# Modulation of two transformer blocks: four of six weight thirds multiplied and added on VectorE, with one sum over the partitions on TensorE

## The chip, the cores and the metric

The kernel runs on one core of one Trainium2 chip. The metric is the device time of one execution in microseconds (us), from the launch of the program to its end. A span is the time from the first to the last instruction of a profiled execution, a little shorter than the execution's own time.

## What is computed

The program is two transformer blocks on 256 tokens of 1024 features, in float32. The first block is a gated feed-forward, an attention mixer and a second gated feed-forward. The second block is two layers over the token stream and a context stream of 256 tokens. Each of its layers has normalisations that are scaled and shifted by a modulation, three branches (Fourier, window attention and a gated recurrence), a gated merge of the branches, and a feed-forward with squared ReLU. The change touches the modulation:

```python
def modulation(cond, w, b):
    m = jax.nn.silu(cond) @ w + b
    return jnp.split(m, 6, axis=-1)

for l in range(DEPTH_2):
    mx = [m[:, None, :] for m in modulation(c, w_mod[l], b_mod[l])]
    mc = modulation(c_ctx, w_mod[l], b_mod[l])
    h = adaln_norm(x, norm1_g[l], mx[0], mx[1])
    ...
    x = x + mx[2] * y
    h2 = adaln_norm(x, norm2_g[l], mx[3], mx[4])
    x = x + mx[5] * sq_relu_mlp(h2, w_ff1[l], w_ff2[l])
```

For each of the two layers, two vectors of 1024 (one for the tokens, one for the context) are multiplied with a weight of 1024 x 6144. That is 25 MB of weights per layer that are read once, for two rows of output. The kernel splits the 6144 columns of a layer into three thirds of 2048 columns (r = 0, 1, 2), so there are six thirds (l, r).

## The kernel before

**The large products.** Every weight of the large matmuls comes in units of 128 partitions x 1024 elements. `wunit` (L230 to L237) loads a unit into `raw` on the queue of SyncE (SP), ScalarE (ACT) rounds it into `hi` (L235), and VectorE (DVE) subtracts to get the remainder `lo` (L236). Each of the three tiles has three buffers. `mm3` (L239 to L242) makes each product out of three matmuls on TensorE (PE): high times high, low of the weight and low of the activation in turn. A unit is 24 matmuls, of 512 columns where both streams are computed together and of 256 where only one is. A unit's `hi` buffer comes free when TensorE has finished the unit three places before it.

**The modulation.** `mods` (L670 to L701) is a generator that is given a list of thirds. A third is eight steps. A step loads 128 rows of the third, a tile `wm` of 128 x 2048 with two buffers (L679), and multiplies it by the 128 rows of silu(cond), padded from 2 to 32 columns in `csil32`. The 2048 columns are four quarters of 512, each a matmul of a 32-column block of the array (L681), and the eight steps add up in one PSUM bank. After the eighth step the bank is copied to SBUF (L686), transposed (L689), and added to the bias into `modt` (L691). Where it is needed, `derived` (L699) is made of it. `csil` holds the two vectors as 128 x 8 x 2.

**Where the steps stand.** The callers pull one step at a time between their own products, with `next(between, None)`. Third (0,0) runs in the first feed-forward, at about 60 us. Thirds (0,1) and (0,2) run in `merge` of layer 0 (L1303, L1318, L1332), which goes over n = 0, 1, 2 (the branches) and over jb = 0 to 3: for n = 0 and 1 a gate product of 2 units of 256 columns (the context's gate has been computed ahead), a branch product of 1 unit of 512 columns, and multiplications by the gate on VectorE (L888, L1337, L1339, L1340). The three thirds of layer 1 run in layer 0's feed-forward (L1395 to L1455), which is two halves hf, each a first product `w_ff1` (L1422, L1434) and a second, `w_ff2` (L1450). Two steps are pulled before the feed-forward and one or two at each unit pair of `w_ff1`.

**What lies between merge and feed-forward.** The product with `w_out` (L1385, L1390) is made for both streams for jb = 0, 1, and for the context (s = 1) and then the tokens (s = 0) for jb = 2, 3. As soon as a stream is done, its modulated normalisation `adaln` (L460 to L473) runs: the sum of squares on TensorE (L326, L357), VectorE and GpSimd for the reciprocal root (L365, L368), diagonals (L378, L380), a matmul that spreads them over the partitions (L381), and then for each of 8 feature blocks L469 and L472 on VectorE and L471 on ScalarE. The context's `adaln` runs while TensorE makes the `w_out` product of the tokens, and `w_ff1` begins with the context.

**The order.** The program is recorded in the order of the code, and a scheduler of the Tile framework then orders the instructions of each engine. Each engine works through its own queue in order. An instruction that waits holds up all that stands behind it on the same engine, and this holds for the DMA issues on SP's queue too.

## Time and profile before

| | |
|---|---|
| time, median of 3 runs | 2091.83 us (2088.09 to 2098.27) |
| the profiled execution's own time | 2091.31 us |
| its span | 2089.2 us |
| TensorE busy, matmuls | 2039.9 us |
| VectorE busy | 1292.0 us |
| ScalarE busy | 1060.4 us |
| moved by DMA | 328.04 MB, mean 157 GB/s |
| granted clock of TensorE | 0.991 |

The busy time of an engine is the time in which at least one of its instructions is at work. The granted clock is a share of full speed. A stretch is given below by its start and end in us from the span's start: the merge of layer 0 is 905 to about 1085, `w_out` and `adaln` 1085 to 1165, and its feed-forward 1129 to about 1500.

### The profile page before, as it was taken

Reading aid. Unit: us, or ns where it says so; the run is one execution under the profiler, and the core shown is the slowest. Engines: PE = TensorE matmul, PEld = TensorE weight load, DVE = VectorE, ACT = ScalarE, POOL = GpSimd, SP = SyncE. Lnnn points to the kernel's source line nnn. Section 1 sums busy time; section 2 is a strip of 40 time slices with the busy share of each in tenths; the row PEclk is TensorE's granted clock in tenths of the full one; section 3 lists DMA queues with packets and bytes.
Section 4 is the critical chain, followed back from the end, with each engine's and each line's share of the span. In section 5 each row is a group of like instructions: output and inputs, shape, how many; then the busy total and the mean of one; then the engine's idle time right before and its main releaser. Section 6 shows DMA issues by size and latency. Waiting matters only on the chain.

```text
span 2089.2 us, 34286 instructions
## 1 busy us (share of the span) xinstructions
PE 2039.9 (98%) x13959; PEld 1802.4 (86%) x13959; DVE 1292.0 (62%) x2011; ACT 1060.4 (51%) x1716; POOL 69.4 (3%) x63
## 2 busy tenths in 40 slices
PE   8999999999999999999999999999999999999999
PEld 8899988999999777888778778778898678999998
DVE  5575666865667699855456433343478897666654
ACT  5354455644446588664444331233266775555542
POOL 1111000111000000000000000000000000000000
PEclk9999999999999999999999999999999899999999
DMA  7886654566562211168535763342363123655564
GB/s 230 295 247 199 183 163 136 174 183 187 171 206 71 71 41 51 54 226 272 188 141 173 261 224 108 111 152 91 109 184 110 43 74 121 199 174 153 182 186 136
DMA packets 294687, 328.04 MB, mean 157 GB/s; under 512 B 18816, under 2 KB 282834, under 8 KB 287874
## 3 DMA queue, kind: packets, MB, share of 16 engines
q1 hardware_dynamic: 294530, 325.86, 49.7%
q8 instruction: 109, 1.79, 0.4%
q14 instruction: 48, 0.39, 0.1%
HBM read 318.40 MB, written 11.35 MB: 158 GB/s over the span
## 4 chain that ended last, share of the span: by engine, by line
PE 91%; DVE 3%; ACT 3%; DMA 1%; issue 1%; POOL 0%; SPq 0%; POOLq 0%; DVEq 0%; ACTq 0%
PE mx L240 14%; PE mx L242 14%; PE mx L241 14%; PE mm L240 12%; PE mm L242 12%; PE mm L241 12%; PE hg L1187 2%; PE ax L681 1%; PE at L1036 1%; PE ax L326 1%; PE mx L681 1%; PE at L1073 1%; PE at L1063 1%; PE at L240 1%; PE at L242 1%; PE at L241 1%
## 5 line engine op out<-in xcount | busy, mean ns | idle before, releaser
L236 DVE TENSOR_TENSOR lo<-raw,hi 128x1024 fp32r<-128x1024 f32 x478 | 584.8, 1225 | 511.0 <-ACT hi L235 507.0
L235 ACT CAST hi<-raw 128x1024 fp32r<-128x1024 f32 x478 | 497.3, 1041 | 716.1 <-PE mx L241 390.7
L240 PE MATMUL mx<-hh,hi 128*128 128x256 f32 (+1 forms) x1248 | 379.6, 304 | 1.2 <-ACT hh L400 1.2
L242 PE MATMUL mx<-hh,lo 128*128 128x256 f32 (+1 forms) x1248 | 376.9, 302 | 0.6 <-DVE lo L236 0.6
L241 PE MATMUL mx<-hl,hi 128*128 128x256 f32 (+1 forms) x1248 | 376.6, 302 | 0.5 <-DVE hl L401 0.5
L240 PE MATMUL mm<-hh,hi 128*128 128x256 f32 (+1 forms) x1136 | 371.7, 327 | 4.9 <-ACT z L1127 1.7
L242 PE MATMUL mm<-hh,lo 128*128 128x256 f32 (+1 forms) x1136 | 367.5, 324 | 1.5 <-DVE lo L236 1.5
L241 PE MATMUL mm<-hl,hi 128*128 128x256 f32 (+1 forms) x1136 | 365.9, 322 | 0.3 <-DVE hl L472 0.3
L240 PEld LDWEIGHTS mx<-hh,hi 128*128 128x128 f32 x1248 | 235.5, 189 | 25.4 <-ACT hi L235 6.7
L242 PEld LDWEIGHTS mx<-hh,lo 128*128 128x128 f32 x1248 | 236.4, 189 | 10.6 <-DVE lo L236 1.0
L241 PEld LDWEIGHTS mx<-hl,hi 128*128 128x128 f32 x1248 | 236.2, 189 | 10.4 <-DVE hl L401 0.8
L240 PEld LDWEIGHTS mm<-hh,hi 128*128 128x128 f32 x1136 | 215.3, 190 | 32.3 <-issue 7.4
L242 PEld LDWEIGHTS mm<-hh,lo 128*128 128x128 f32 x1136 | 215.2, 190 | 18.3 <-DVE lo L236 2.6
L241 PEld LDWEIGHTS mm<-hl,hi 128*128 128x128 f32 x1136 | 215.8, 190 | 16.4 <-issue 2.5
L240 PE MATMUL mx<-fh,hi 128*128 128x256 f32 (+1 forms) x368 | 120.3, 327 | 0.0
L241 PE MATMUL mx<-fl,hi 128*128 128x256 f32 (+1 forms) x368 | 120.3, 327 | 0.0
L242 PE MATMUL mx<-fh,lo 128*128 128x256 f32 (+1 forms) x368 | 120.2, 327 | 0.0
L240 PEld LDWEIGHTS mx<-fh,hi 128*128 128x128 f32 x368 | 69.2, 188 | 6.8
L241 PEld LDWEIGHTS mx<-fl,hi 128*128 128x128 f32 x368 | 69.2, 188 | 6.6
L242 PEld LDWEIGHTS mx<-fh,lo 128*128 128x128 f32 x368 | 69.4, 188 | 6.4
L1187 PE MATMUL hg<-qt,kt 128*128 128x128 f32 x384 | 62.0, 285 | 1.0 <-ACT dg L1194 0.5
L1187 PEld LDWEIGHTS hg<-qt,kt 128*128 128x128 f32 x384 | 55.2, 197 | 7.7 <-issue 2.1
(380 smaller groups left out, 3732.6 us busy)
## 6 DMA issues: line engine op xcount, KB each, us to landing
raw<-in_w_ff_dram SPq DMA_DIRECT2D x136, 512.0 KB
raw<-in_w_in_dram SPq DMA_DIRECT2D x130, 512.0 KB
wm<-in_w_mod_dram SPq DMA_DIRECT2D x48, 1024.0 KB
raw<-in_ffn_w_gate_dram SPq DMA_DIRECT2D x44, 512.0 KB
raw<-in_ffn_w_up_dram SPq DMA_DIRECT2D x44, 512.0 KB
raw<-in_ffn_w_down_dram SPq DMA_DIRECT2D x40, 512.0 KB
raw<-in_w_out_dram SPq DMA_DIRECT2D x28, 512.0 KB
raw<-in_w_qkv_dram SPq DMA_DIRECT2D x24, 512.0 KB
```

What stands on the lines that cost most here:

```text
L235: S.copy(hi, raw)
L236: V.tensor_tensor(out=lo, in0=raw, in1=hi.bitcast(F32), op=ALU.subtract)
L240: PE.matmul(ps, l[0], r[0], start=start, stop=False)
L241: PE.matmul(ps, l[0], r[1], start=False, stop=False)
L242: return PE.matmul(ps, l[1], r[0], start=False, stop=stop)
L326: PE.matmul(self.ss[:, t:t + 1], sq[:, i * T + t * P:i * T + (t + 1) * P], ones[:, :1], start=(first and i == 0 and t == 0), stop=(last an ...
L681: PE.matmul(ps[32 * c:32 * c + 32, :], cst_[:, k, :], wm[:, c * 512:(c + 1) * 512], start=(k == 0), stop=(k == KD - 1), tile_position=(0, ...
L1036: PE.matmul(scs[t], q[e][:, t * P:(t + 1) * P], kd[g][i][:, 512 - nk:], start=(i == 0), stop=(i == 1 and s == 1))
L1063: PE.transpose(pt[:, kt * T + t * P:kt * T + (t + 1) * P], sb[:, c0:c0 + P], ident)
L1073: mm = PE.matmul(op[e * 64:e * 64 + 64, :T], vt[:, vc:vc + 64], pts[e][:, kt * T:(kt + 1) * T], start=(ki == 0), stop=(ki == nk // P - 1))
L1187: PE.matmul(ps[:, (s * 2 + st) * P:(s * 2 + st + 1) * P], kt[:, s * T + st * P:s * T + (st + 1) * P], qt[:, s * T + tt * P:s * T + (tt + 1 ...
```

## The change

Each third in a list now has a flag. Without it the eight steps are matmuls as before. With it, a step is two VectorE instructions, one for each of the two vectors s: the first step multiplies `wm` by the vector's 128 values, one per partition, into an accumulator `macc` of 128 x 2048 (L700), and the seven others multiply and add to it in place (L702). After the eighth step two groups of four matmuls add the accumulators up over the 128 partitions, with a column of ones in `pick` that puts each vector's sum into its row (L686). Copy, transposes and bias are as before (now L710, L713, L715, L723). Thirds (0,2), (1,0), (1,1) and (1,2) have the flag; (0,0) and (0,1) have not.

The places at which steps are pulled change as well. In `merge` the second pull of a jb is at n = 0 alone, so that third (0,1) is done in n = 0, and third (0,2) has four steps in n = 1 and four in n = 2. In the feed-forward the two steps ahead of it and the four in the first `w_ff1` products are gone. One step is pulled at each of the six other unit pairs of the first half, three after each of the four jb of its `w_ff2`, and one at each of the first six pairs of the second half.

```diff
--- before.py
+++ after.py
@@ -667,21 +667,45 @@
     derived = [[[cp.tile([P, 8], F32, name=f"der{l}{s}{i}") for i in range(2)] for s in range(2)] for l in range(2)]
 
 
+
+    pick = cp.tile([P, 2, 32], F32, name="pick")
+    nc.gpsimd.memset(pick, 0.0)
+    for s in range(2):
+        nc.gpsimd.memset(pick[:, s, s:s + 1], 1.0)
+
     def mods(pool, parts, tag="ax"):
+
+
 
         cst_ = pool.tile([P, KD, 32], F32, tag="csil32", name="csil32")
         nc.gpsimd.memset(cst_, 0.0)
         nc.gpsimd.tensor_copy(cst_[:, :, 0:2], csil)
-        for l, r in parts:
-            ps = bank(tag)
+
+        def quarters(ps, stat, mov, first, final):
+            for c in range(4):
+                PE.matmul(ps[32 * c:32 * c + 32, :], stat, mov[:, c * 512:(c + 1) * 512], start=first, stop=final,
+                          tile_position=(0, 32 * c))
+
+        for l, r, dve in parts:
+            ps = None if dve else bank(tag)
+            acc = [pool.tile([P, 2048], F32, tag=f"macc{s}", name="macc") for s in range(2)] if dve else None
             for k in range(KD):
                 wm = pool.tile([P, 2048], F32, tag="wm", name="wm", bufs=2)
                 nc.sync.dma_start(out=wm, in_=a["w_mod_2"][l, k * P:(k + 1) * P, r * 2048:(r + 1) * 2048])
-                for c in range(4):
-                    PE.matmul(ps[32 * c:32 * c + 32, :], cst_[:, k, :], wm[:, c * 512:(c + 1) * 512],
-                              start=(k == 0), stop=(k == KD - 1), tile_position=(0, 32 * c))
+                if not dve:
+                    quarters(ps, cst_[:, k, :], wm, k == 0, k == KD - 1)
+                for s in range(2 if dve else 0):
+                    c = csil[:, k, s:s + 1]
+                    if k == 0:
+                        V.tensor_scalar(out=acc[s], in0=wm, scalar1=c, scalar2=None, op0=ALU.mult)
+                    else:
+                        V.scalar_tensor_tensor(out=acc[s], in0=wm, scalar=c, in1=acc[s], op0=ALU.mult, op1=ALU.add)
                 if k < KD - 1:
                     yield
+            if dve:
+                ps = bank(tag)
+                for s in range(2):
+                    quarters(ps, pick[:, s], acc[s], s == 0, s == 1)
             sb = tmp(512, "sq", 3)
             V.tensor_copy(sb, ps)
             pt = bank(tag)
@@ -768,7 +792,7 @@
         logc = btmp("sb")[:8, :]
         nc.sync.dma_start(out=logc, in_=a["c_logc"])
         nc.sync.dma_start(out=two(namask), in_=a["c_namask"])
-        steps = mods(bp, [(0, 0)])
+        steps = mods(bp, [(0, 0, False)])
         for _ in range(3):
             next(steps)
             yield
@@ -1300,7 +1324,7 @@
         mp = mg.enter_context(tc.tile_pool(name=f"mg{l}", bufs=1, reuse_waits="tile"))
         merged = mp.tile([P, 4 * ns, 512], F32, name="merged")
 
-        between = mods(mp, [(0, 1), (0, 2)]) if l == 0 else iter(())
+        between = mods(mp, [(0, 1, False), (0, 2, True)]) if l == 0 else iter(())
 
         def merge(n):
             parts = []
@@ -1329,7 +1353,7 @@
                         sigmoid_(e, g, -1.0)
                         sg.append(two(e))
                 pps = linear(a["w_branch_2"][l, n], 0, 4, jb * 256, bact, ntok)
-                if jb % 2:
+                if n == 0:
                     next(between, None)
                 for i, pr in enumerate(pps):
                     mu = two(merged[:, jb * len(pps) + i, :])
@@ -1392,10 +1416,7 @@
                 adaln(x, (s,), A2, B2, h, sums)
 
         fp = fs.enter_context(tc.tile_pool(name=f"ff{l}", bufs=1, reuse_waits="tile"))
-        between = mods(fp, [(1, 0), (1, 1), (1, 2)], "mx") if l == 0 else iter(())
-
-        for _ in range(2):
-            next(between, None)
+        between = mods(fp, [(1, r, True) for r in range(3)], "mx") if l == 0 else iter(())
         if last:
             h = [pair(k) for k in range(KD)]
             adaln(x, streams, A2, B2, h, sums)
@@ -1420,7 +1441,6 @@
                 for s in (1, 0):
                     for j in range(2):
                         [ps] = linear(a["w_ff1_2"][l], 0, KD, j * 256, of(hboth, s), T)
-                        next(between, None)
                         r = fp.tile([P, 512], F32, tag="r", name="r", bufs=2)
                         S.activation(r, ps, AF.Relu)
                         r2 = fp.tile([P, 512], F32, tag="r", name="r", bufs=2)
@@ -1432,7 +1452,7 @@
                             V.tensor_tensor(out=lo, in0=r2[:, c], in1=hi.bitcast(F32), op=ALU.subtract)
             for j in range(len(hid) // 2, n_h):
                 pss = linear(a["w_ff1_2"][l], 0, KD, (hf * n_h + j) * 256, hx if last else hboth, ntok)
-                for _ in range(2 if hf == 0 else j < 4):
+                if hf == 0 or j < 6:
                     next(between, None)
                 for q, ps in enumerate(pss):
                     r = fp.tile([P, 512], F32, tag="r", name="r", bufs=2)
@@ -1449,6 +1469,8 @@
             for jb in range(4 if last or hf == 0 else 3):
                 residual(linear(a["w_ff2_2"][l], hf * kh * P, kh, jb * 256, fact, ntok), jb, 5,
                          sums if hf == ns - 1 else None)
+                for _ in range(3 if hf == 0 else 0):
+                    next(between, None)
                 if last:
                     store(fp, jb)
         for _ in between:
```

Three places in VectorE's queue show where the scheduler has put the new instructions. First, `merge` with n = 1, from the branch product of jb = 1 to that of jb = 2 (`mm` and `mx` are banks that TensorE fills, `lo` the remainders of the next units). Before:

```order
L1339 TENSOR_TENSOR sg_10820<-mx_10907,sg_10820 128x2x256
L1340 TENSOR_TENSOR merged_10214<-merged_10214,sg_10820 128x512
L236 TENSOR_TENSOR lo_11031<-raw_11028,hi_11030 128x1024
L236 TENSOR_TENSOR lo_11068<-raw_11065,hi_11067 128x1024
L236 TENSOR_TENSOR lo_11098<-raw_11095,hi_11097 128x1024
L888 TENSOR_SCALAR sg_10949<-sg_10949 128x512
L888 TENSOR_SCALAR sg_11062<-sg_11062 128x512
L1339 TENSOR_TENSOR sg_10949<-mm_11026,sg_10949 128x2x256
```

Now:

```order
L702 SCALAR_TENSOR_TENSOR macc_10795<-wm_11019,csil_138,macc_10795 128x2048
L1363 TENSOR_TENSOR sg_10845<-mm_10920,sg_10845 128x2x256
L1363 TENSOR_TENSOR sg_10845<-mx_10921,sg_10845 128x2x256
L1364 TENSOR_TENSOR merged_10218<-merged_10218,sg_10845 128x512 x2
L702 SCALAR_TENSOR_TENSOR macc_10796<-wm_11019,csil_138,macc_10796 128x2048
L912 TENSOR_SCALAR sg_10956<-sg_10956 128x512
L236 TENSOR_TENSOR lo_11036<-raw_11033,hi_11035 128x1024
L236 TENSOR_TENSOR lo_11073<-raw_11070,hi_11072 128x1024
L236 TENSOR_TENSOR lo_11103<-raw_11100,hi_11102 128x1024
```

One accumulation stands ahead of the gate multiplications and one between them and the next three remainders. Second, the end of `w_out` for the context and the start of its `adaln`. Before:

```order
L236 TENSOR_TENSOR lo_12063<-raw_12060,hi_12062 128x1024
L1374 SCALAR_TENSOR_TENSOR big_11698<-mx_11910,modt0_139,big_11698 128x256 x2
L236 TENSOR_TENSOR lo_12099<-raw_12096,hi_12098 128x1024
L365 TENSOR_SCALAR rvs_11987<-ax_11974 128x2
L378 TENSOR_SCALAR diag_11991<-cmain_72,rss_11989 128x128
L469 SCALAR_TENSOR_TENSOR sq_11997<-big_11698,der011_144,ax_11986 128x256
```

Now:

```order
L702 SCALAR_TENSOR_TENSOR macc_12564<-wm_12806,csil_138,macc_12564 128x2048
L1398 SCALAR_TENSOR_TENSOR big_11696<-mx_11908,modt0_139,big_11696 128x256 x2
L236 TENSOR_TENSOR lo_12097<-raw_12094,hi_12096 128x1024
L236 TENSOR_TENSOR lo_12127<-raw_12124,hi_12126 128x1024
L365 TENSOR_SCALAR rvs_11985<-ax_11972 128x2
L702 SCALAR_TENSOR_TENSOR macc_12565<-wm_12806,csil_138,macc_12565 128x2048
L378 TENSOR_SCALAR diag_11989<-cmain_72,rss_11987 128x128
L1398 SCALAR_TENSOR_TENSOR big_11696<-mm_12027,modt0_139,big_11696 128x256 x2
L469 SCALAR_TENSOR_TENSOR sq_11995<-big_11696,der011_144,ax_11984 128x256
```

An accumulation stands ahead of the residual that ends the context's `w_out`, another between L365 and L378, and a second remainder has moved ahead of L365; before, it stood near the end of the `adaln`. In TensorE's queue the spreading matmul L381 of this `adaln` stood 23 plain matmuls behind the first sum of squares (L326), and now stands 65 behind it, with 31 left of the 96 that the tokens' `w_out` has there. Third, `w_ff2` of the feed-forward's first half, around the residual of jb = 1. Before:

```order
L236 TENSOR_TENSOR lo_13312<-raw_13309,hi_13311 128x1024
L236 TENSOR_TENSOR lo_13348<-raw_13345,hi_13347 128x1024
L236 TENSOR_TENSOR lo_13378<-raw_13375,hi_13377 128x1024
L1362 SCALAR_TENSOR_TENSOR big_11698<-mx_13217,modt0_139,big_11698 128x256 x2
L1362 SCALAR_TENSOR_TENSOR big_11698<-mm_13218,modt0_139,big_11698 128x256 x2
L236 TENSOR_TENSOR lo_13408<-raw_13405,hi_13407 128x1024
```

Now:

```order
L236 TENSOR_TENSOR lo_13239<-raw_13236,hi_13238 128x1024
L702 SCALAR_TENSOR_TENSOR macc_13138<-wm_13274,csil_138,macc_13138 128x2048
L702 SCALAR_TENSOR_TENSOR macc_13139<-wm_13274,csil_138,macc_13139 128x2048
L702 SCALAR_TENSOR_TENSOR macc_13138<-wm_13278,csil_138,macc_13138 128x2048
L702 SCALAR_TENSOR_TENSOR macc_13139<-wm_13278,csil_138,macc_13139 128x2048
L236 TENSOR_TENSOR lo_13287<-raw_13284,hi_13286 128x1024
L1386 SCALAR_TENSOR_TENSOR big_11696<-mx_13144,modt0_139,big_11696 128x256 x2
L236 TENSOR_TENSOR lo_13317<-raw_13314,hi_13316 128x1024
L702 SCALAR_TENSOR_TENSOR macc_13138<-wm_13408,csil_138,macc_13138 128x2048
L1386 SCALAR_TENSOR_TENSOR big_11696<-mm_13145,modt0_139,big_11696 128x256 x2
L236 TENSOR_TENSOR lo_13347<-raw_13344,hi_13346 128x1024
```

Between one remainder and the next there are now up to four accumulations, where there were none. In all queues, the order of compute instructions ahead of 905 us and behind 1510 us is as before.

## Rows read from the trace of the kernel before

**Rows 1.** The page: busy time by engine, and the chain's shares by engine.

```profile
PE 2039.9 (98%) x13959; PEld 1802.4 (86%) x13959; DVE 1292.0 (62%) x2011; ACT 1060.4 (51%) x1716; POOL 69.4 (3%) x63
...
PE 91%; DVE 3%; ACT 3%; DMA 1%; issue 1%; POOL 0%; SPq 0%; POOLq 0%; DVEq 0%; ACTq 0%
```

**Rows 2.** Windows: stretch, length, busy per engine (instructions), granted clock, DMA share, GB/s.

```profile
905.00:962.00 57.00, 57.00 (x376) 46.51 (x375) 31.08 (x41) 34.83 (x54) 0.51 (x2) 1.00 0.80 279
962.00:1009.00 47.00, 47.00 (x298) 37.80 (x298) 26.02 (x35) 22.11 (x32) 0.00 (x0) 1.00 0.77 254
...
1085.00:1165.00 80.00, 78.34 (x551) 68.21 (x550) 51.35 (x87) 35.87 (x57) 1.38 (x2) 1.00 0.60 201
1165.00:1255.00 90.00, 90.00 (x441) 64.01 (x440) 36.97 (x50) 30.03 (x41) 0.00 (x0) 1.00 0.69 246
1255.00:1345.00 90.00, 90.00 (x388) 72.39 (x387) 26.52 (x33) 16.78 (x16) 0.00 (x0) 1.00 0.31 97
1345.00:1450.00 105.00, 105.00 (x463) 80.95 (x462) 43.52 (x50) 37.80 (x50) 0.00 (x0) 1.00 0.40 130
```

**Rows 3.** Timeline of TensorE: start, duration, instruction; 256 columns, then 512.

```profile
937.46 0.28 PE L241 MATMUL mx<-hl,hi 128*128 128x256 f32 x1
937.58 0.28 PE L242 MATMUL mx<-hh,lo 128*128 128x256 f32 x1
...
1184.66 0.39 PE L240 MATMUL mm<-hh,hi 128*128 128x512 f32 x1
...
1191.42 0.40 PE L242 MATMUL mm<-hh,lo 128*128 128x512 f32 x1
```

**Rows 4.** Timeline of TensorE in the feed-forward: modulation steps, in pairs and alone.

```profile
1205.00 1.92 PE L681 MATMUL mx<-wm,csil 128*32 128x512 f32 x16
...
1218.25 1.92 PE L681 MATMUL mx<-wm,csil 128*32 128x512 f32 x16
...
1348.04 1.06 PE L681 MATMUL mx<-wm,csil 128*32 128x512 f32 x8
...
1360.43 1.06 PE L681 MATMUL mx<-wm,csil 128*32 128x512 f32 x8
```

**Rows 5.** Line L681 alone: all of it, then its share of a window (TensorE, weight loads).

```profile
L681 PE MATMUL ax<-wm,csil x192: 590/593/617, 66.2 to 1060.2; 128*32 128x512 f32 x192
...
L681 PE MATMUL mx<-wm,csil x192: 592/592/617, 1129.2 to 1499.7; 128*32 128x512 f32 x192
...
962.00:1009.00 47.00, 5.33 (x40) 0.79 (x40) 1.00 0.77 254
```

**Rows 6.** Groups of VectorE by line and shape: count, busy us, mean ns, idle before.

```profile
L236 DVE TENSOR_TENSOR lo<-raw,hi 128x1024 fp32r<-128x1024 f32 x470 | 579.0, 1233 | 503.2 <-ACT hi L235 499.1 <-PE ax L989 1.6 <-issue 0.3
...
L1137 DVE SCALAR_TENSOR_TENSOR gt<-z,gt 128x512 f32<-128x512 f32 x16 | 10.9, 683 | 0.1
...
L1141 DVE TENSOR_SCALAR gt<-z,lbol 128x512 f32<-128x512 f32 x16 | 7.6, 477 | 0.0
...
L1052 DVE TENSOR_SCALAR sb<-sb,den 128x256 f32<-128x256 f32 x16 | 4.9, 345 | 0.0
```

**Rows 7.** Timeline of all engines near 1130 us, in w_out of the tokens.

```profile
1129.16 1.92 PE L681 MATMUL mx<-wm,csil 128*32 128x512 f32 x16
...
1129.95 1.21 DVE L236 TENSOR_TENSOR lo<-raw,hi 128x1024 fp32r<-128x1024 f32 x1
```

**Rows 8.** Timeline of TensorE and VectorE: the context's adaln, its spread and its end.

```profile
1122.41 0.71 PE L381 MATMUL ax<-diag,cmain 128*128 128x128 f32 x4 [0.16 <-DVE diag L378]
...
1131.08 0.87 DVE L472 SCALAR_TENSOR_TENSOR hl<-sq,modt,hh 128x256 fp32r<-128x256 f32 x2
```

**Rows 9.** Timeline of VectorE in the first half's w_ff2: one remainder.

```profile
1276.20 1.22 DVE L236 TENSOR_TENSOR lo<-raw,hi 128x1024 fp32r<-128x1024 f32 x1 [4.38 <-ACT hi L235]
```

**Rows 10.** Timeline of SP and TensorE near 60 us: the first modulation weights.

```profile
58.78 1.94 SPq L679 DMA_DIRECT2D wm<-in_w_mod_dram  x2
...
66.22 1.06 PE L681 MATMUL ax<-wm,csil 128*32 128x512 f32 x8 [1.44 <-DMA wm<-in_w_mod_dram]
```

## Prediction

> **What bounds the kernel now.** I read the page first, then windows over the stretches that change, then the timeline inside them. On the page TensorE is busy 98% of the span and holds 91% of the chain that ended last [rows 1]. The reader is to see in the windows that TensorE is busy for the whole of every changed stretch but the one around `adaln`, while VectorE is busy between 29% and 64% and DMA at most 80% [rows 2]. A busy engine can still be one whose instructions wait inside. Against that speaks the timeline: two matmuls of 256 columns start 0.12 us apart, and 30 in a row of 512 columns start 6.76 / 29 = 0.233 us apart [rows 3]. Twice the columns take twice the time, while a unit asks ScalarE and VectorE for the same work in both cases; so the columns set the pace, not the preparation of the weights. The granted clock is 1.00 in all these windows. What TensorE is spared there comes off the time, as long as VectorE delivers `lo` in time.
>
> **What is removed.** 32 of the 48 modulation steps leave TensorE. Line L681 has 384 records, 8 per step [rows 5]. The price is read from the period of equal work in the feed-forward. 48 matmuls of 0.233 us are 11.2 us. With a pair of steps between them the period is 1218.25 - 1205.00 = 13.25 us, with one step alone 1360.43 - 1348.04 = 12.39 us [rows 4]. So a pair costs 2.05 us and a single 1.19 us. On the timeline the removed steps are 8 of third (0,2) and 8 of layer 1 alone, and 8 pairs: 16 x 1.19 + 8 x 2.05 = 35.4 us.
>
> **What is added to TensorE.** Each of four thirds ends in two groups of four matmuls of the same shape, priced as a pair: 4 x 2.05 = 8.2 us. Net -27.2 us, all on the path. Copy, transposes and bias stay. The memsets for `pick` lie on GpSimd, which is busy 3% [rows 1]: 0.
>
> **What is added to VectorE.** No row has 2048 elements. An addition or multiply-add of two tensors takes 683 ns at 512 elements and 1233 ns at 1024, 1.07 ns per element more; that gives 1233 + 1024 x 1.07 = 2330 ns. A product with one value per partition takes 345 ns at 256 and 477 ns at 512, so 477 + 1536 x 0.52 = 1270 ns [rows 6]. A third is 14 x 2.33 + 2 x 1.27 = 35.2 us, the four 141 us. As a whole this has cover: the windows leave VectorE 21 to 64 us each [rows 2]. Only local lack counts, in three places.
>
> - Merge, n = 1 (962 to 1009). VectorE has 26.0 us of work; two first products and six multiply-adds bring 16.5, together 42.5. TensorE has 47.0 less 5 single steps (5.33 us of records [rows 5], 5 x 1.19 = 6.0), 41.0. So VectorE is the longer by 1.5 us, and one accumulation stands ahead of the next branch's `lo`. I take +2; 0 to 5, since busy times side by side can overlap, or stack up late.
> - The context's `adaln`. From its spread to its last `hl` VectorE needs 1122.41 to 1131.95 = 9.5 us [rows 8]. The spread now stands 42 matmuls later, and 31 are left before `w_ff1` begins, 3.7 us. `w_ff1` needs the last block only 4.0 us after its start. 9.5 - 7.7 = 1.8; I take +2. At the lower end 0, because one `lo` has moved ahead of the chain; at the upper 5, the whole delay of 42 x 0.12.
> - `w_ff2` of the first half. A remainder starts 4.38 us after VectorE came free, in a period of 5.60 [rows 9]; a unit's `hi` is made when the third unit before it is done, so `lo` has two units, 11.2 us, less 2.3 for both conversions, 8.9. Four accumulations in a row are 9.3, a residual 0.9. I take +2; 0 to 5.
>
> One gain could be none: the pair at 1129 us ran where TensorE would have waited for a `lo` that started at 1129.95 [rows 7]. That `lo` stands ahead of the `adaln` now; 0, at most +1.8.
>
> **What is moved.** The number of loads is the same. Merge with n = 0 has 8 steps instead of 6, so 2 MB more: 279 GB/s x 57 us = 15.9 MB become 17.9 in 59.4 us, 301 GB/s, at a DMA share of 0.80 x 301 / 279 = 0.86 [rows 2]. Still below 1; 0, with the share as the cover. On SP's queue a load of `wm` now waits for the second VectorE instruction two steps back, and the `raw` loads behind it wait too. In the order those are needed some ten VectorE instructions later, over 8 us; 0.
>
> **Sum.** The profiled execution took 2091.3 us, half a microsecond below the median of the runs. 2091.3 - 27.2 + 2 + 2 + 2 = 2070.1; I say 2070.
>
> **Rivals.**
> - *All of it stays* (2062 to 2066): the three local terms are 0, 2064.1. For it, the scheduler has spread most accumulations over VectorE's idle time; against it, the three places above.
> - *VectorE becomes the bound in merge and in the clusters of the feed-forward* (2080 to 2091): each of the 32 steps costs TensorE 0.35 to 0.85 us, 11 to 27 us back. For it, 42.5 against 41.0 us in n = 1; against it, 61.7 of 90 us in `w_ff2`, 26.5 + 35.2.
> - *Slower*: in VectorE's queue the multiply-add that waits for `wm` stands ahead of `lo`. The place is where steps stand in a row, as in `w_ff2`. The first `wm` took 66.22 - 58.78 = 7.4 us from issue to use [rows 10], and with two buffers only the 4.7 us of the step between are covered, so 2.8 us of standing per step; if 16 steps pass that to TensorE, 45 us: 2091.3 - 27.2 + 45 = 2109. It decides from 27.2 / 32 = 0.85 us per step on. For it, the queue is in order; against it, the 8.9 us that a `lo` has, and a DMA share of 0.31 there [rows 2] where the 7.4 us are from the crowded start.
> - *TensorE is not what the stretches wait for* (2088 to 2092): the matmuls' starts are held by the weight loads or by `hi` and `lo`, and the removed steps turn into waiting, so the saving is at most some 3 us. Against it, the spacing of rows 3. The Trainium skill, Perfetto Trace Analysis, section Identifying the Most-Contended Engine, says that matmul busy time is no good measure of nearness to the limit, and wants LDWEIGHTS busy. By that page the 86% of weight loading [rows 1] would leave 14% slack, and about 0.86 x 27.2 = 23 us of the net would count, an estimate that would give 2074. The trace does not follow it here: starts are as far apart as the columns are long.
>
> **How the numbers follow.** The forecast, 2066 to 2080, has 0.64; all of it 0.10; VectorE the bound 0.16; slower 0.06; TensorE not the bound 0.04. Half a per cent, about 10.5 us, is what a measurement of this kernel can tell from no change: faster means below 2081.4, slower above 2102.3. Faster is 0.64 + 0.10 + 0.02 of the VectorE case = 0.76. Within is 0.14 + 0.04 + 0.01 = 0.19. Slower is 0.05. The range goes from 2062, where every local term is 0 and the runs' scatter helps, to 2086, half into the VectorE case; the upper bounds of all four terms together (16.8 us) give 2080.9.
>
> **What would show it.** Right: TensorE busy falls by about 27 us to 2013, VectorE rises to about 1430, L702 takes near 2.33 us and L700 near 1.27; a period of two `w_ff1` units in the first half is 11.2 us instead of 13.25; the waits of TensorE for `lo` L236 and for `hh`/`hl` between 962 and 1345 grow from almost nothing to about 6 us. Wrong: L702 well over 2.4 us, TensorE waiting over 11 us for `lo` in these stretches, VectorE waiting for `wm` ahead of a `lo`, or a granted clock below 1.00 where TensorE now stands idle.

## The result, and the profile after

| | before | after |
|---|---|---|
| time, median of 4 runs | 2092.32 us (2088.09 to 2098.27) | 2061.77 us (2060.80 to 2063.32) |
| span of the profiled execution | 2089.2 us | 2060.4 us |
| TensorE busy | 2039.9 us | 2010.5 us |
| VectorE busy | 1292.0 us | 1420.1 us |

The change made the kernel faster: the ratio of the times is 0.9855, with a 95% interval of 0.9838 to 0.9872, and the medians are 30.5 us apart. The forecast was 2070 us and a range of 2062 to 2086; the time lies 0.2 us below the range.

The page after, busy time by engine and shares of the chain, answers to [rows 1]:

```profile
PE 2010.5 (98%) x13767; PEld 1796.7 (87%) x13767; DVE 1420.1 (69%) x2075; ACT 1061.6 (52%) x1716; POOL 73.9 (4%) x66
...
PE 91%; DVE 3%; ACT 3%; DMA 1%; issue 1%; POOL 0%; POOLq 0%; SPq 0%; DVEq 0%; ACTq 0%
```

TensorE has 192 records fewer (256 of the modulation left, 64 for the sums came) and is as full as before. The windows of the changed stretches, columns as in [rows 2]:

```profile
905.00:960.00 55.00, 55.00 (x357) 42.96 (x359) 26.40 (x37) 32.14 (x51) 0.00 (x0) 1.00 0.84 297
960.00:1003.00 43.00, 43.00 (x285) 38.65 (x278) 42.17 (x47) 24.01 (x33) 0.00 (x0) 1.00 0.79 267
1003.00:1064.00 61.00, 61.00 (x263) 49.09 (x262) 46.19 (x46) 25.38 (x35) 0.00 (x0) 1.00 0.47 153
1073.00:1150.00 77.00, 74.52 (x506) 68.10 (x505) 68.25 (x99) 36.02 (x57) 4.84 (x4) 1.00 0.61 202
1150.00:1236.00 86.00, 86.00 (x385) 69.85 (x385) 54.73 (x54) 32.88 (x46) 0.00 (x0) 1.00 0.48 156
1236.00:1330.00 94.00, 94.00 (x423) 73.11 (x422) 72.97 (x64) 19.18 (x20) 0.00 (x0) 1.00 0.61 202
1330.00:1430.00 100.00, 100.00 (x439) 79.17 (x438) 64.86 (x65) 34.38 (x45) 0.00 (x0) 1.00 0.41 136
```

The second row is the one to look at: VectorE is busy for 42.2 of 43 us, and TensorE still for all of them. Only the row around `adaln` (1073 to 1150) has idle time on TensorE, as before. The two new instructions, each line alone:

```profile
L702 DVE SCALAR_TENSOR_TENSOR macc<-wm,csil,macc x56: 2342/2346/2353, 970.7 to 1368.6; 128x2048 f32<-128x2048 f32 x56
...
L700 DVE TENSOR_SCALAR macc<-wm,csil x8: 1277/1278/1286, 961.4 to 1317.2; 128x2048 f32<-128x2048 f32 x8
```

The prices drawn out from shorter rows [rows 6] were 2.33 and 1.27 us; measured are 2.346 and 1.278.

**Where the time went.** I cut the span at five starts on TensorE's timeline: the first product of merge, the first sum of squares after `w_out` (L326), the first 512-column product of `w_ff1`, the sum of squares that ends the feed-forward, and the first product of layer 1. The same cuts serve for all runs below (us; in engine_only two units change places at the third cut, so its two stretches stand as one sum):

| run | merge, w_out | to 512-col. w_ff1 | rest of feed-forward | to layer 1 | layer 1 | span |
|---|---|---|---|---|---|---|
| before | 211.88 | 49.11 | 345.66 | 17.59 | 559.3 | 2089.2 |
| the change | 204.42 | 43.52 | 332.58 | 16.20 | 557.8 | 2060.4 |
| again | 204.43 | 43.38 | 332.58 | 16.17 | 558.0 | 2060.3 |
| places_only | 211.88 | 46.25 | 354.04 | 17.24 | 559.8 | 2094.4 |
| engine_only | 203.81 | 389.50 in both | | 16.17 | 558.0 | 2071.6 |
| late_end | 204.84 | 44.54 | 332.57 | 16.17 | 559.5 | 2062.2 |
| free_adaln | 204.46 | 42.64 | 332.59 | 16.16 | 559.5 | 2059.6 |
| merge_only | 204.42 | 49.11 | 345.65 | 16.19 | 558.2 | 2079.1 |
| doubled | 215.24 | 52.96 | 377.73 | 16.23 | 559.9 | 2126.1 |
| five_thirds | 200.03 | 54.28 | 332.58 | 16.53 | 557.6 | 2065.1 |
| half_third | 207.12 | 44.15 | 332.60 | 16.29 | 565.6 | 2071.2 |
| five_free | 199.87 | 42.62 | 332.59 | 16.20 | 558.3 | 2054.3 |
| five_late | 197.69 | 42.63 | 332.58 | 16.17 | 559.3 | 2055.3 |

The change and `again` are the same program, and their stretches ahead of layer 1 agree to 0.14 us, where the times of whole runs scatter by 2 to 10 us. It is the only program that was profiled twice. From before to after it is -7.46, -5.59, -13.08, -1.39 and -1.5 us, and +0.2 ahead of merge. By the prices of [rows 4] the steps that left are worth 8 x 1.19 - 2.05 = 7.47 in merge, 2.05 + 4 x 1.19 = 6.81 around `adaln`, and 7 x 2.05 + 4 x 1.19 - 3 x 2.05 = 12.96 in the rest of the feed-forward. So merge and feed-forward kept all, `adaln` gave 1.2 us back, and 2.9 us came from stretches that the change does not touch (1.39 and 1.5).

**The 2.9 us.** Behind the feed-forward, ScalarE and TensorE in the timeline, before (first fence) and after (second), and a window of before (third):

```profile
1528.03 1.04 ACT L235 CAST hi<-raw 128x1024 fp32r<-128x1024 f32 x1 [2.44 <-DMA raw<-in_w_in_dram]
1528.98 0.72 ACT L352 ACTIVATE sq<-big 128x256 f32<-128x256 f32 x2
...
1529.44 0.61 PE L357 MATMUL ax<-cmain,sq 128*128 128x1 f32 x4 [2.02 <-ACT sq L352]
```

```profile
1500.69 1.05 ACT L235 CAST hi<-raw 128x1024 fp32r<-128x1024 f32 x1 [1.04 <-PE mx L241]
1501.65 0.72 ACT L352 ACTIVATE sq<-big 128x256 f32<-128x256 f32 x2
...
1502.11 0.61 PE L357 MATMUL ax<-cmain,sq 128*128 128x1 f32 x4 [0.61 <-ACT sq L352]
```

```profile
1531.00:1535.00 4.00, 4.00 (x23) 4.00 (x23) 1.58 (x3) 0.40 (x1) 0.69 (x1) 0.60 0.94 295
```

Before, a weight's cast waits for its load; the squares stand behind it in ScalarE's queue, TensorE waits 2.02 us for them, and the granted clock is 0.60 in the four microseconds from 1531. After, the cast waits only for its buffer, and the load, issued 3.9 us earlier, is there; before it took 5.3 us from issue to cast. That is the 1.39 us.

The 1.5 us of layer 1 go with the clock. Over the first seven microseconds of layer 1 the granted clock is 0.76 in before, places_only, late_end, free_adaln, doubled and five_late, where layer 1 takes 559.3 to 559.9 us; it is 1.00 in the other six, where it takes 557.6 to 558.3 (half_third is apart). It does not need the late load: in free_adaln (first line) and in engine_only (second) TensorE waits 0.59 us for the squares.

```profile
1500.10:1507.10 7.00, 7.00 (x48) 7.00 (x48) 3.50 (x8) 1.95 (x4) 1.61 (x1) 0.76 1.00 343
1513.60:1520.60 7.00, 6.90 (x57) 6.73 (x58) 4.66 (x10) 2.92 (x6) 1.62 (x1) 1.00 0.99 346
```

Why the clock fell in one and not in the other is open.

### The profile page after: what moved, and what is told of

It is laid out like the page before. It is cut to its first block, busy times and chain, and to the rows that moved or that the text cites. A ratio compares the mean times of both kernels' runs of the same rounds, so it can differ in the third digit from the quotient of the medians.

```text
span 2060.4 us, 33976 instructions
## 1 busy us (share of the span) xinstructions
PE 2010.5 (98%) x13767; PEld 1796.7 (87%) x13767; DVE 1420.1 (69%) x2075; ACT 1061.6 (52%) x1716; POOL 73.9 (4%) x66
## 4 chain that ended last, share of the span: by engine, by line
PE 91%; DVE 3%; ACT 3%; DMA 1%; issue 1%; POOL 0%; POOLq 0%; SPq 0%; DVEq 0%; ACTq 0%
PE mx L240 14%; PE mx L242 14%; PE mx L241 14%; PE mm L240 12%; PE mm L242 12%; PE mm L241 12%; PE hg L1211 2%; PE at L1060 1%; PE at L1097 1%; PE ax L326 1%; PE at L240 1%; PE at L242 1%; PE at L241 1%; PE at L1087 1%; PE ax L686 1%; DVE lo L236 1%
## 5 line engine op out<-in xcount | busy, mean ns | idle before, releaser
L242 PEld LDWEIGHTS mx<-hh,lo 128*128 128x128 f32 x1248 | 236.5, 190 | 10.7 <-DVE lo L236 1.0
L702 DVE SCALAR_TENSOR_TENSOR macc<-wm,csil,macc 128x2048 f32<-128x2048 f32 x56 | 130.5, 2346 | 0.2 <-DMA wm<-in_w_mod_dram 0.2
```

The costliest lines, as they stand in the source:

```text
L242: return PE.matmul(ps, l[1], r[0], start=False, stop=stop)
L702: V.scalar_tensor_tensor(out=acc[s], in0=wm, scalar=c, in1=acc[s], op0=ALU.mult, op1=ALU.add)
```

## The experiments

My theory after the result: what counts is columns off TensorE, nearly in full; VectorE's idle time covers the accumulations; the places of the steps serve VectorE's margin and save nothing by themselves. Rivals: the places bring part of the gain; the margin is wide; the 2.9 us belong to the change.

**places_only: the new places, all thirds on TensorE.**

```diff
-        between = mods(mp, [(0, 1, False), (0, 2, True)]) if l == 0 else iter(())
+        between = mods(mp, [(0, 1, False), (0, 2, False)]) if l == 0 else iter(())
...
-        between = mods(fp, [(1, r, True) for r in range(3)], "mx") if l == 0 else iter(())
+        between = mods(fp, [(1, r, False) for r in range(3)], "mx") if l == 0 else iter(())
```

> All six thirds stay on TensorE (all flags False), only the places at which steps are pulled are those of the change. Theory (the saving is the columns that leave TensorE): the places save nothing; the 40 steps that are pulled are 28 singles and 4 groups of three, 28 x 1.19 + 4 x 2.91 = 45 us against 24 singles and 8 pairs, 45 us, in the kernel before. Expected 2089 to 2094 us, with TensorE busy near 2040. Rival (the places bring a good part of the gain, by lifting steps out of the stretch around adaln and out of the end of the feed-forward): 2075 to 2086.

Measured: 2097.44 us, ratio 1.0028 (1.0016 to 1.0041), 4 to 6 us slower than before and outside what I gave. Three of the four groups of three came out as a pair and a single, the fourth as three singles: 18 singles and 3 pairs of steps in the rest of the feed-forward, 27.6 us against 19.1, and the table has +8.4. Around `adaln`, where no step stands now, the stretch is only 2.9 us shorter though 6.8 us of steps are gone. Two waits of TensorE, in its timeline, took their place:

```profile
1130.72 0.39 PE L242 MATMUL mx<-hh,lo 128*128 128x256 f32 x1 [1.75 <-DVE lo L236]
...
1150.18 0.42 PE L240 MATMUL mx<-hh,hi 128*128 128x256 f32 x1 [2.46 <-ACT hi L235]
```

So most of the time of the steps around `adaln` had stood where TensorE waits anyway. The places alone cost time; VectorE's part at these places is worth 2097.4 - 2061.8 = 35.6 us.

**engine_only: the four thirds on VectorE, at the places of before.** The hunks that move a `next(between, None)` are undone:

```diff
-                if n == 0:
+                if jb % 2:
...
+        for _ in range(2):
+            next(between, None)
...
+                        next(between, None)
...
-                if hf == 0 or j < 6:
+                for _ in range(2 if hf == 0 else j < 4):
...
-                for _ in range(3 if hf == 0 else 0):
-                    next(between, None)
```

> The four thirds on VectorE as in the change, but pulled at the places of the kernel before: two steps (9.4 us of accumulations) at each unit pair of w_ff1 in the first half, where VectorE has some 5 us of its own in 11.2 us. Theory (VectorE's margin is thin and the places were needed): VectorE is over-full by some 3 us in each of six periods, of which the scheduler can shift only what the two wm buffers allow; 2068 to 2080, with TensorE waiting for lo at 1166 to 1230. Rival (the margin is wide, places don't matter): 2060 to 2065.

Measured: 2077.12 us, ratio 0.9923 (0.9907 to 0.9939), as the theory had it: the places are worth 15 us to the change by the medians, 11 by the profiled spans. Against the change the two feed-forward stretches are 389.50 - 376.10 = 13.4 us longer, and merge is not. VectorE and TensorE in `w_ff1`:

```profile
1186.16 9.13 DVE L702 SCALAR_TENSOR_TENSOR macc<-wm,csil,macc 128x2048 f32<-128x2048 f32 x4
...
1198.01 2.36 DVE L236 TENSOR_TENSOR lo<-raw,hi 128x1024 fp32r<-128x1024 f32 x2
...
1199.28 0.80 PE L242 MATMUL mm<-hh,lo 128*128 128x512 f32 x1 [3.03 <-DVE lo L236]
```

Four accumulations stand in a row, `w_ff1`'s own work (L1467, L1468) follows, and `lo` comes 3.03 us late. In all TensorE waits 11.5 us in the two stretches, 6.3 for `lo` and 3.4 for `hi`, against 2.2 us in the change. So rows ahead of `lo` are not the only path: one cast waits 5.68 us, until 1189.46, for a load that SP issued at 1183.04, behind two `wm` loads that took its queue from 1176.75 to 1181.61. How the 13.4 us divide between the two paths was not tested.

**late_end: the last two steps of (1,2) at the end, as before** (`j < 6` becomes `j < 4`).

> The change, with the last two steps of third (1,2) pulled after the second half of w_ff2, as in the kernel before, instead of ahead of it. It tests the 2.9 us that layer 1 gained though nothing in it was changed: in the trace of before a hi cast waited 1.4 us for its load behind the end of the feed-forward, held the squares of adaln behind it on ScalarE, and TensorE's granted clock was low for 4 us after its wait of 2.0 us. If the late steps caused that: 2064 to 2066, with TensorE waiting about 2 us for the squares. If the landing of that load varies between executions: 2060 to 2064.

Measured: 2064.37 us, ratio 0.9866 (0.9848 to 0.9884), no difference from the change that this can tell. The time lies between the two forecasts; the wait decides: TensorE waits 0.6 us for the squares, so in this profile the late end did not make the load late.

**free_adaln: no accumulation of layer 1 ahead of the context's last block.** At step k = 0 of third (1,0), a zero multiple of that block is added to `csil`:

```diff
+                if dve and (l, r, k) == (1, 0, 0):
+                    V.scalar_tensor_tensor(out=csil.rearrange("p k s -> p (k s)"), in0=late[0], scalar=0.0,
+                                           in1=csil.rearrange("p k s -> p (k s)"), op0=ALU.mult, op1=ALU.add)
...
+        if l == 0:
+            late[0] = h[KD - 1][1].bitcast(F32)[:, T:T + 16]
```

> The change, with the first accumulation of third (1,0) made to depend on the last block that the context's adaln writes, so that no accumulation can stand among the residuals and the adaln at 1085 to 1150 us. Theory (that stretch lost 1.5 to 2 us to accumulations that stand ahead of adaln's chain): 2059 to 2061, the stretch from w_out to the 512-column w_ff1 shorter by 1.5 to 2 us. Rival (the loss there is not from accumulations, or comes back where they now stand): 2061 to 2065.

Measured: 2061.83 us, ratio 0.9852 (0.9837 to 0.9867), the time of the change, as the rival had it. The stretch is 0.9 us shorter, 42.64, not 1.5 to 2; a wait of 1.75 us for `lo` remains that no accumulation causes.

**merge_only: (0,2) on VectorE, layer 1's thirds as before.** The feed-forward's part of the diff above, and

```diff
-        between = mods(fp, [(1, r, True) for r in range(3)], "mx") if l == 0 else iter(())
+        between = mods(fp, [(1, r, False) for r in range(3)], "mx") if l == 0 else iter(())
```

> Third (0,2) alone on VectorE, at the change's places in merge; the three thirds of layer 1 on TensorE at the places of the kernel before. Theory (each third's worth is its steps less its sum): merge shorter by eight singles less one pair, 7.5 us, as in the change; the rest as before; 2084 to 2087 against 2092 to 2093. It also shows once more the hi cast that waits for its load behind the end of the feed-forward: if that is tied to modulation steps on TensorE in the feed-forward, TensorE waits about 2 us for the squares of adaln again, as in the two kernels that had them; if the load's landing only varies, the wait may be 0.6 us.

Measured: 2082.00 us, ratio 0.9957 (0.9943 to 0.9972), 2 us below what I gave. Merge is 204.42 us as in the change, the feed-forward 345.65 as before: the parts add up. TensorE waits 0.6 us for the squares although the feed-forward has its modulation matmuls, so in this profile the late load does not come with them.

**doubled: every accumulation made twice.**

```diff
                         V.scalar_tensor_tensor(out=acc[s], in0=wm, scalar=c, in1=acc[s], op0=ALU.mult, op1=ALU.add)
+                        V.scalar_tensor_tensor(out=acc[s], in0=wm, scalar=pick[:, 1, 0:1], in1=acc[s], op0=ALU.mult, op1=ALU.add)
```

> The change, with every accumulation made twice: a second one multiplies the same tile by a column of zeros and adds, 2.35 us more for each of 64, 150 us more of VectorE, nothing more on TensorE. It asks where VectorE's cover ends. From the windows of the change, busy time and what is added against the length of the stretch: merge n = 1 42 + 14 in 43, n = 2 46 + 19 in 70, w_out and adaln 68 + 16 in 77, first w_ff1 55 + 18 in 86, first w_ff2 73 + 33 in 94, second w_ff1 65 + 33 in 100. Theory (cover counts per stretch, and only work beyond a stretch's length costs): 13 + 8 + 12 = 33 us more, 2085 to 2105, the loss in these three stretches alone. Rival (each accumulation in a full stretch delays lo at once): far more, over 2115. Rival (wide margin): under 2075.

(The first products, L700, are not followed by one: there are 56 more, 131 us, and not the 64 and 150 us that I had reckoned with.) Measured: 2130.53 us, ratio 1.0184 (1.0169 to 1.0200): the rival. A window of `w_ff2`, and in it VectorE and TensorE:

```profile
1239.00:1355.00 116.00, 98.28 (x419) 76.39 (x421) 99.27 (x75) 19.01 (x19) 0.00 (x0) 0.91 0.48 157
```

```profile
1288.23 4.61 DVE L702 SCALAR_TENSOR_TENSOR macc<-wm,csil,macc 128x2048 f32<-128x2048 f32 x2
1292.75 4.61 DVE L703 SCALAR_TENSOR_TENSOR macc<-wm,pick,macc 128x2048 f32<-128x2048 f32 x2
...
1298.55 0.80 PE L242 MATMUL mx<-fh,lo 128*128 128x512 f32 x1 [10.68 <-DVE lo L236]
```

VectorE is busy for 86% of this window and TensorE waits 10.7 us at once; from merge to the end of the feed-forward its waits for `lo` add up to 43 us. The sum of work against the length of a stretch does not foretell this; the rows of accumulations in VectorE's queue do.

**five_thirds and half_third: more off TensorE.** The first puts all of (0,1) on VectorE:

```diff
-        between = mods(mp, [(0, 1, False), (0, 2, True)]) if l == 0 else iter(())
+        between = mods(mp, [(0, 1, True), (0, 2, True)]) if l == 0 else iter(())
...
-                if n == 0:
+                if jb == 1 or (n, jb) == (2, 3):
```

The second puts k = 4 to 7 of (0,1) there, at the change's places (`own` is the number of steps on TensorE, 4 for this third, and its first product stands at k = `own`):

```diff
-                if not dve:
+                if k < own:
                     quarters(ps, cst_[:, k, :], wm, k == 0, k == KD - 1)
-                for s in range(2 if dve else 0):
+                for s in range(2 if k >= own else 0):
...
-                    quarters(ps, pick[:, s], acc[s], s == 0, s == 1)
+                    quarters(ps, pick[:, s], acc[s], s == 0 and not own, s == 1)
```

> Third (0,1) on VectorE too, its and (0,2)'s 16 steps pulled as 5, 5 and 6 over merge's n = 0, 1, 2. TensorE is spared 7.5 us more. VectorE then has 118 + 35 = 153 us of work in a merge of 163 us, and the stretch n = 1 with five steps has 28 + 23 = 51 in 41. Theory (cover counts per stretch): 5 to 10 us come back, 2060 to 2066, no gain over the change. Rival (the scheduler levels it over the whole merge): 2054 to 2057.

Measured: 2068.16 us, ratio 0.9889 (0.9872 to 0.9905), above both ranges. Merge is 4.4 us shorter than in the change, and the stretch of `adaln` 10.8 longer. Windows there, and an accumulation and a late sum in the timeline:

```profile
1121.00:1128.00 7.00, 6.59 (x31) 6.62 (x32) 4.61 (x8) 1.21 (x3) 1.60 (x1) 0.50 0.33 88
1142.00:1148.00 6.00, 6.00 (x30) 6.00 (x30) 6.00 (x4) 1.44 (x2) 0.00 (x0) 0.51 0.78 242
```

```profile
1108.59 2.34 DVE L702 SCALAR_TENSOR_TENSOR macc<-wm,csil,macc 128x2048 f32<-128x2048 f32 x1
...
1120.57 0.69 DVE L341 TENSOR_TENSOR acc<-acc,sq 128x512 f32<-128x512 f32 x1
...
1121.41 0.77 PE L326 MATMUL ax<-cmain,acc 128*128 128x1 f32 x3 [1.65 <-DVE acc L341]
...
1141.68 0.58 PE L242 MATMUL mm<-hh,lo 128*128 128x256 f32 x1 [4.86 <-DVE lo L236]
```

> Third (0,1) half on each: k = 0 to 3 as matmuls, k = 4 to 7 accumulated on VectorE in n = 0, the sums added into the same bank. TensorE is spared four singles less a pair, 4.8 - 2.05 = 2.7 us; VectorE has 26 + 16.5 = 43 us in a stretch of 50. Theory: there is cover, 2058 to 2060. Rival (lo is delayed where accumulations bunch up): 2061 to 2065.

Measured: 2069.48 us, ratio 0.9893 (0.9877 to 0.9909), 10 us above the theory's range and above the rival's too. Merge is 2.7 us longer than in the change instead of 2.7 shorter. VectorE and TensorE in n = 0 in the timeline, and a window behind it with the clock:

```profile
943.38 4.61 DVE L704 SCALAR_TENSOR_TENSOR macc<-wm,csil,macc 128x2048 f32<-128x2048 f32 x2
...
948.50 4.60 DVE L704 SCALAR_TENSOR_TENSOR macc<-wm,csil,macc 128x2048 f32<-128x2048 f32 x2
953.02 0.75 DVE L914 TENSOR_SCALAR sg<-sg 128x512 f32<-128x512 f32 x2
953.69 1.22 DVE L236 TENSOR_TENSOR lo<-raw,hi 128x1024 fp32r<-128x1024 f32 x1
...
954.96 0.49 PE L242 MATMUL mm<-brh,lo 128*128 128x512 f32 x1 [2.65 <-DVE lo L236]
```

```profile
956.00:959.00 3.00, 3.00 (x9) 2.33 (x8) 3.00 (x2) 1.13 (x2) 0.00 (x0) 0.51 0.81 265
```

Two rows of 4.6 us with one product between them put `lo` 2.65 us late. The other 7.8 us lie in layer 1 (565.6 us), in the profile of the slowest of its four runs (2073.03 us). Part of them is the clock, here over the first seven microseconds of layer 1, where the change has 1.00:

```profile
1505.60:1512.60 7.00, 7.00 (x35) 7.00 (x35) 1.88 (x5) 0.40 (x1) 1.61 (x1) 0.51 0.99 348
```

Why the clock fell, and the rest, are open.

**again, five_free and five_late: the change once more, and two versions to beat it.** The last two join (0,1) on VectorE and the hold of free_adaln (not shown again). five_free keeps the places of five_thirds; five_late spreads merge's steps as 4, 4 and 8:

```diff
-        between = mods(mp, [(0, 1, False), (0, 2, True)]) if l == 0 else iter(())
+        between = mods(mp, [(0, 1, True), (0, 2, True)]) if l == 0 else iter(())
...
-                if n == 0:
+                if n == 2:
                     next(between, None)
```

> The changed kernel itself once more, for what varies between executions: the time of a hi cast's load behind the end of the feed-forward (the wait of TensorE for the squares of adaln was 2.0 and 1.7 us in two kernels, 0.6 to 0.9 in five) and the stretches of low granted clock in layer 1. Expected 2060 to 2064; if the 1.4 us that the change gained at that load are an effect of the change, the wait is 0.6 us again; if they vary, either is possible. The rest of layer 1 took 557.8 us after that place in the profile of the change and 558.0 to 559.8 in the others: 557.5 to 560 is expected.

> Third (0,1) on VectorE as in five_thirds (5, 5 and 6 steps in merge's n = 0, 1, 2), and third (1,0) held back until the context's adaln has written its last block, as in free_adaln. In five_thirds merge was 4.4 us shorter than in the change, and w_out with adaln 10.8 longer, with one wait of 4.9 us for lo and the clock at half after it. Theory (those 10.8 are accumulations of third (1,0) that stand ahead of lo in VectorE's queue): they go, 2056 to 2059, better than the change. Rival (they come from what merge left over for later): 2063 to 2070.

> As five_free, with the 16 steps of merge as 4, 4 and 8 over n = 0, 1, 2. By the windows of the change VectorE then has 26 + 19 = 45 us in the 48 of n = 0, 45 in the 41 of n = 1 and 65 in the 70 of n = 2. Theory (where the steps fit, no lo is late): merge 5 to 7 us shorter than in the change, 2054 to 2058. Rival (bunched accumulations delay lo wherever VectorE is over 90% busy): 2059 to 2066.

Measured on one chip: again 2063.17 us, ratio 0.9864 (0.9848 to 0.9881); five_free 2056.59, 0.9834 (0.9819 to 0.9848); five_late 2056.48, 0.9829 (0.9815 to 0.9844). five_late beats both kernels: some 7 us below the change, and its interval lies below that of again. five_free differs from five_thirds by the hold alone, and the stretch of `adaln` falls from 54.28 to 42.62 us: the 10.8 were accumulations of third (1,0). The windows of merge in five_late:

```profile
907.00:960.00 53.00, 53.00 (x345) 48.27 (x345) 50.27 (x49) 36.56 (x56) 0.00 (x0) 1.00 0.87 297
960.00:1001.00 41.00, 40.48 (x253) 34.59 (x252) 40.22 (x46) 21.36 (x29) 0.00 (x0) 1.00 0.81 266
1001.00:1064.00 63.00, 63.00 (x271) 50.68 (x270) 59.24 (x54) 28.26 (x40) 0.00 (x0) 1.00 0.58 191
```

VectorE is 94 to 98% busy throughout, and TensorE loses 0.5 us: merge is 6.7 us shorter than in the change, of 7.5 that its steps are worth. It is also 2.2 us shorter than in five_free, and yet the two times are equal: in five_late's profile merge begins 2.2 us later and layer 1 takes 1.0 us longer, where the kernels do not differ.

## Why the prediction was right or wrong

- **Direction and net, right.** 27.2 us net off TensorE were forecast; without the 1.2 us around `adaln` the three stretches gave 7.46 + 6.8 + 13.08 = 27.3. TensorE busy fell to 2010.5 (forecast about 2013), VectorE rose to 1420 (about 1430). The rival that TensorE is not the bound falls. Its estimate by the Trainium skill, Perfetto Trace Analysis, section Identifying the Most-Contended Engine, was 23 us; the trace does not follow it: merge gave 7.46 of 7.47 us, with weight loading busy for 80 to 82% of it before (86% of the span).
- **The merge term, mis-sized: +2, measured 0**, because a row was misread. The window 962 to 1009 begins 4 us after n = 1 does and ends 1 us before its end, but all eight accumulations of n = 1 were added to it. The whole of n = 1, before (first line) and after (second):

```profile
958.12:1010.12 52.00, 52.00 (x336) 42.29 (x332) 28.11 (x38) 23.55 (x34) 0.51 (x2) 1.00 0.77 254
960.69:1006.80 46.11, 46.11 (x297) 41.71 (x294) 45.32 (x48) 24.76 (x35) 0.00 (x0) 1.00 0.82 279
```

  Five modulation steps leave it, so TensorE should need 52.0 - 5 x 1.19 = 46.0 us, and 46.1 were measured; VectorE should need 28.1 + 16.5 = 44.6, and 45.3 were measured. So VectorE was not the longer by 1.5 us. The stretch was nearly full, no long row stood ahead of a `lo`, and TensorE waited for none.
- **The w_ff2 term, mis-sized: +2, measured 0.** The four accumulations in a row exist. VectorE and ScalarE after the change:

```profile
1254.61 9.13 DVE L702 SCALAR_TENSOR_TENSOR macc<-wm,csil,macc 128x2048 f32<-128x2048 f32 x4
1263.66 1.22 DVE L236 TENSOR_TENSOR lo<-raw,hi 128x1024 fp32r<-128x1024 f32 x1
...
1257.05 1.05 ACT L235 CAST hi<-raw 128x1024 fp32r<-128x1024 f32 x1 [4.54 <-PE mm L241]
```

  I had set all 9.3 us against the 8.9 that a `lo` has. But the row began 2.4 us before that unit's `hi` did and 3.5 before it was done, so only 1263.66 - 1258.10 = 5.6 us of it stood between `hi` and `lo`. In engine_only a row as long cost 3.03 us, with four more instructions behind it and ahead of `lo`; there, by the order of casts and remainders, the whole row stood behind the unit's `hi`, done at 1182.62.
- **The adaln term: +2, measured +1.2, and near by luck.** It was to come as a wait of `w_ff1` for the last block of the context's `adaln`. TensorE waits there for no `hh` or `hl`. Its idle time in this stretch grew from 1.7 us (49.11 less 47.45 busy) to 2.5 (43.52 less 41.04): 0.49 us for a sum of squares, 0.51 for a diagonal (0.50 before), and the longest, 1.20 us (0.78 in `again`), for a cast that itself waited 0.71 us for its load:

```profile
1142.09 0.39 PE L240 MATMUL mx<-hh,hi 128*128 128x256 f32 x1 [1.20 <-ACT hi L235]
```

  What makes up the whole 1.2 us is open: in free_adaln TensorE is idle for 2.9 us there, and the stretch is 0.9 us shorter. The forecast also asked whether the pair at 1129 us had covered a wait for `lo` [rows 7], "0, at most +1.8", and took 0. places_only and free_adaln have a wait of 1.75 us at that place, so the cover was real in the order of before; the change has no wait for a `lo` there, as I had argued.
- **DMA in n = 0, right**: 0.84 and 297 GB/s (0.86 and 301 forecast).
- **A term put at nothing: 2.9 us outside the changed stretches.** The load behind the feed-forward was late in the profiles of before and places_only (waits of 2.0 and 1.7 us) and in none of eleven others (0.6 to 0.9), merge_only with the same steps at the same places of the feed-forward among them. These two are also the only kernels without a third on VectorE, so that the change plays a part is not excluded. The low clock at the start of layer 1 is found in versions of the change too (late_end, free_adaln, five_late). No program was seen both ways, so that these parts vary between executions is likely and not shown.
- **One rival does not add up.** "VectorE becomes the bound" gives 11 to 27 us back, which from 2064.1 is 2075 to 2091 and not 2080 to 2091.
- **The failed step** is the sum of local terms, +6 for what is +1.2: I put VectorE's lack at 2 us in each of three places from sums of busy time, and expected some 6 us of waits for `lo`, `hh` and `hl` between 962 and 1345; there were none, and 2.2 us of others. "All of it stays" had 0.10. With +1.2 the sum gives 2065.3; the 2.9 us outside make up nearly all that is left to the profiled execution's 2062.2. Either miss alone would have left the time inside the range; together they put the median 0.2 us below it.

## What to carry to other kernels

In this kernel an engine at 98% of a stretch took work off a saturated neighbour and cost nothing, as long as its queue held no long row of that work between the input and the result that the neighbour waits for next; so cost such a move by the rows in the queue, from the moment the input is there, take windows that hold the whole stretch, and spread the steps by which stretch has room. Work removed where the bounding engine waits anyway gives back less than its price. The scheduler put accumulations ahead into a stretch that was tight: a false dependency on the last instruction of the tight chain held them back, and was worth 11.7 us once a fifth third had moved.

## What the runs showed of the hardware

- After some waits TensorE runs at its lower level (1.2 GHz) for a few microseconds. Granted clocks of 0.60, 0.57, 0.51, 0.50 and 0.51 stand in windows at or behind the end of waits of 2.02, 2.46, 2.65, 3.03 and 4.86 us (before, places_only, half_third, engine_only, five_thirds). The length of the wait does not tell it: 0.50 also came with the 1.65 us at 1121.41 in five_thirds, and 0.76 with 0.59 us in free_adaln, while after the 1.75 us of free_adaln and 0.59 us of engine_only it was 1.00. So a late `lo` can cost more than its own wait.
- A load of 512 KB that is used 3.9 us after its issue was there in eleven profiles and late in two, by 1.4 and 1.1 us, with the same loads and casts around it.
- The first product of a third (one value per partition times a 128 x 2048 tile) takes 1.28 us; the multiply-add, which also reads the accumulator, takes 2.35, 1.8 times as long.
